# Inverse rows kept in a PSUM bank while VectorE updates them, with one PSUM bank fewer for the recurrence's transposes

## The chip, the core and the metric

The kernel runs on one core of a Trainium2 chip. A core has five engines, each with an instruction queue of its own that runs in order: TensorE (PE in the profile; PEld is its weight load), VectorE (DVE), ScalarE (ACT), GpSimd (POOL) and SyncE (SP), which here only issues DMAs. Tensors lie in device memory (HBM), in SBUF (128 partitions) or in PSUM, of which this kernel uses eight banks of 128 partitions with 512 float32 each. TensorE writes its results to PSUM, from which VectorE and ScalarE read them.

The metric is the device time of one execution in microseconds. Lower is better. The time before is the median of three timed runs; the profile is of a further execution.

## The reference, cut to what matters

One layer of a hybrid decoder for one sequence of 1024 tokens, model width 1024, all float32. A modulated RMSNorm feeds one input projection to 3360 columns, which serves two mixers: an RWKV-7 recurrence of 8 heads (64 wide) and latent attention of 8 heads. Their gated outputs go through one output projection, a residual and a last norm. The change lies in the recurrence:

```python
def step(state, inp):
    r_t, w_t, k_t, v_t, kk_t, a_t = inp
    sa = jnp.einsum('bhvk,bhk->bhv', state, kk_t)
    state = (state * w_t[:, :, None, :]
             - sa[..., None] * (kk_t * a_t)[:, :, None, :]
             + v_t[..., None] * k_t[:, :, None, :])
    y = jnp.einsum('bhvk,bhk->bhv', state, r_t)
    return state, y
...
y = group_norm_heads(y, lnx_w, lnx_b)
y = y + jnp.sum(rh * kh * r_k.astype(jnp.float32), axis=-1, keepdims=True) * vh
```

Within a chunk of 64 tokens the vectors `sa` of all tokens depend on one another through a lower triangular system with ones on its diagonal. Solving it chunk by chunk replaces the step from token to token, and needs the inverse of one 64 x 64 triangular matrix for each head and chunk.

## The kernel before, in words

**Units.** The recurrence is cut into eight units. A unit is one group of four heads (two pairs `a`, with two heads `s` in the halves of the 128 partitions) and a quarter of the sequence, 256 tokens, which is four chunks. So a unit has 16 combinations of head and chunk, and as many triangular matrices.

**Stages of a unit.** `prep` makes the decayed vectors: `kb` (keys and the removal vectors), `rq` (r and kk). `products` multiplies them on TensorE into the PSUM tiles `gps`; VectorE applies the triangular mask (line 584) and the 32 x 32 diagonal blocks, two per matrix and 32 in all, go to device memory. `invert` (line 613) loads them back so that each of the 128 partitions holds one block, each block being in four partitions, and inverts all 32 blocks at once. A partition keeps 8 of the 32 rows of its block's inverse in `W` (128 x 8 x 32), which starts as rows of the identity, loaded from the input `winit`. For each column `u` from 0 to 30 one VectorE instruction multiplies the `u` entry of each row with row `u` of the block into `wtmp` (line 625) and one subtracts the product from `W` (line 627): 62 instructions a unit, each depending on the one before. `W` then goes to device memory (line 630), `fetch` loads it back in two layouts, and `tmat` builds the off-diagonal block of the full 64 x 64 inverse T with two sets of small matmuls, through the PSUM tiles `y1ps` and `y2ps`. `turn_kb` and `turn_v` transpose the keys and values on TensorE, through the PSUM tiles `tps` and `vps`, and ScalarE copies them out (lines 601, 610, 611). `chain` is the recurrence over the four chunks: short matmuls with ScalarE copies `X`, `ST` and `S` between them. `post` normalises the result and transposes it (`ytps`, copied out by ScalarE in line 770).

**The eight PSUM banks** in this part: two with tag `mm` for the input projection, two with tag `rp` for `prep` and `products`, two with tag `rt`, which `tps`, `vps`, `y1ps`, `y2ps` and `ytps` take in turn (the last unit's `ytps` uses `mm`), and one each for `rc` and `ry`, the chain. A tile that takes a bank waits until the copies out of the tile that had it are done. Before the units begin, a first group of projection tiles borrows `mm`, `rc`, `ry` and both `rt` banks for its accumulators.

**Order of the work.** Stages of several units overlap: a loop over `n` walks through steps and calls the parts of the units at the step numbers in `PREP`, `PROD`, `TURN`, `FETCH`, `TMAT` and `POST`. Between them it issues "filler": the input projection, three matmuls of 128 x 128 x 512 at a time (lines 164 to 166, `mm3`), whose weights are split into a high and a low part by ScalarE and GpSimd (lines 156, 157). A planner then fixes at build time the order of instructions in each engine's queue, from the program's order, from priorities (`tc.high_priority`) and from its own estimates of durations. On the chip the queues run in that order, and each instruction waits for its inputs. Attention and the output projection follow and are not touched.

Of the kernel before, what the change touches and what calls it, by code (L numbers as in the profile page):

```python
# [17 lines left out]
F32 = mybir.dt.float32  # L18
# [3 lines left out]
AF = mybir.ActivationFunctionType  # L22
# [64 lines left out]
def hymba_kernel(ctx: ExitStack, tc: tile.TileContext, x, pos, cols, cst, winit, w_ada, b_gate, w_in, w_lora, w0,  # L87
# [157 lines left out]
    with ExitStack() as s0:  # L245
# [62 lines left out]
        for i in range(4, 8):  # L308
            load_x(i)
        ws.append(load_w(GROUP[2][0], P, st, 3, st))  # L310
        acc = [[(psM if m == 0 else psA).tile([P, HALF], F32, tag=t, name=f"acc{m}{h}", bufs=1 if m == 1 else 2)
                for h, t in enumerate(tags)] for m, tags in enumerate((("mm", "mm"), ("rc", "ry"), ("rt", "rt")))]
        seq = [(0, 0), (1, 0), (0, 1), (1, 1)] + [(kt, h) for kt in range(2, NK) for h in range(2)]
        modulation(0)
        turn_x(*seq[0])
# [276 lines left out]

    def turn_kb(un):

        ps = [psA.tile([P, 8, C], F32, tag="rt", name="tps") for _ in range(2)]
        for c in range(8):
            for s in range(2):
                rows = slice(s * 64, s * 64 + 64)
                T.transpose(ps[s][:, c, :], un["kb"][rows, c, :, :].rearrange("p a t -> p (a t)"), ident[rows, rows])
        for s in range(2):  # L600
            A.activation(un["KB"][:, s], ps[s][:], AF.Copy, scale=col("hs_b" if s else "hs_a"))

    def turn_v(un, q):

        qs = slice(q * 4, q * 4 + 4)
        ps = psA.tile([64, 4, P], F32, tag="rt", name="vps")
        for i in range(4):
            c = q * 4 + i
            T.transpose(ps[:, i, :], un["v"][:, c * C:(c + 1) * C], ident)
        A.copy(un["ST"][64:128, qs, 0, :], ps[:, :, 0:64])  # L610
        A.copy(un["ST"][0:64, qs, 1, :], ps[:, :, 64:128])

    def invert(un):

        i = un["n"]
        N = ch.tile([P, 32, 32], F32, tag="N", name="N", bufs=CB["N"])
        for q in range(4):
            SY.dma_start(N[q * 32:(q + 1) * 32], d_n[i][:])
        W = ch.tile([P, 8, 32], F32, tag="W", name="W")
        SY.dma_start(W[:].rearrange("p i t -> p (i t)"), winit)  # L620
        tp = ch.tile([P, 128], F32, tag="wtmp", name="wtmp")
        for u in range(31):
            n, m = u // 4 + 1, 31 - u
            t = tp[:, :n * m].rearrange("p (i t) -> p i t", i=n)
            V.tensor_tensor(t, W[:, 0:n, u:u + 1].to_broadcast([P, n, m]),  # L625
                            N[:, u:u + 1, u + 1:32].to_broadcast([P, n, m]), ALU.mult)
            V.tensor_tensor(W[:, 0:n, u + 1:32], W[:, 0:n, u + 1:32], t, ALU.subtract)  # L627
        d = d_w[i][:].rearrange("n (i q) t -> q n i t", q=4)
        for q in range(4):
            SY.dma_start(d[q], W[q * 32:(q + 1) * 32])  # L630

    def fetch(un):

# [12 lines left out]
    def tmat(un):  # L646

        GA, TT, T1 = un["GA"], un["TT"], un["T1"]
        ps = psA.tile([P, 8, 32], F32, tag="rt", name="y1ps")
        for c in range(8):  # L650
            for s in range(2):
                a = s * 64
                T.matmul(ps[a + 32:a + 64, c, :], lhsT=GA[s][c // 4][a:a + 32, c % 4, 32:64], rhs=T1[a:a + 32, c, :],
                         start=True, stop=True)
        Y1 = ch.tile([P, 8, 32], F32, tag="Y1", name="Y1")
        A.mul(Y1[32:64], ps[32:64], -1.0)
        V.tensor_scalar(Y1[96:128], ps[96:128], -1.0, None, ALU.mult)
        yield
        ps = psA.tile([P, 8, 32], F32, tag="rt", name="y2ps")
        for c in range(8):  # L660
            for s in range(2):
                a = s * 64
                T.matmul(ps[a:a + 32, c, :], lhsT=Y1[a + 32:a + 64, c, :], rhs=TT[a + 32:a + 64, c, 32:64],
                         start=True, stop=True)
        A.copy(TT[0:32, :, 32:64], ps[0:32])
        V.tensor_copy(TT[64:96, :, 32:64], ps[64:96])

        for q in range(2):
            A.copy(GA[0][q][0:64, :, 0:C], un["rq"][0:64, q * 4:q * 4 + 4, 0, :])
            A.copy(GA[1][q][64:128, :, 0:C], un["rq"][64:128, q * 4:q * 4 + 4, 0, :])  # L670
        yield
# [63 lines left out]
    def post(un):  # L735

        Y = un["Y"]
        ys = evp.tile([P, 8, C], F32, tag="p2", name="ys", bufs=2)
        A.copy(ys[:], Y[:])
        last = un["n"] == 7  # L740

        def fetched(nm, src):
            t = etile(nm) if last else evp.tile([P, HALF], F32, tag="p2", name=nm, bufs=2)
            for a, p, aq in pairs(un):
                SY.dma_start(t[:, aq], src[p][:, un["ts"]])
            return t


        early = [fetched("bv", d_bv), fetched("gr", d_gr)] if last else None
        s1 = evp.tile([P, 8], F32, tag="s1", name="s1")  # L750
        V.tensor_reduce(s1[:], ys[:], AX.X, ALU.add)
        V.tensor_scalar(s1[:], s1[:], 1.0 / C, None, ALU.mult)
        G.tensor_tensor(ys[:], ys[:], s1[:, :, None].to_broadcast([P, 8, C]), ALU.subtract)
        yield
        y2 = evp.tile([P, 8, C], F32, tag="p2", name="y2", bufs=2)
        A.activation(y2[:], ys[:], AF.Square)
        s2 = evp.tile([P, 8], F32, tag="s2", name="s2")
        V.tensor_reduce(s2[:], y2[:], AX.X, ALU.add)
        V.tensor_scalar(s2[:], s2[:], 1.0 / C, GN_EPS, ALU.mult, ALU.add)
        G.tensor_tensor(s2[:], s2[:], col("pw").to_broadcast([P, 8]), ALU.pow)  # L760
        G.tensor_tensor(ys[:], ys[:], s2[:, :, None].to_broadcast([P, 8, C]), ALU.mult)
        yield
        for q in range(2):
            p = 2 * un["g"] + q
            ps = (psM if last else psA).tile([64, 4, P], F32, tag="mm" if last else "rt", name="ytps")
            for i in range(4):
                T.transpose(ps[:, i, :], ys[:, q * 4 + i, :], ident)
            for s in range(2):
                rows = slice(s * 64, s * 64 + 64)
                A.activation(y2[rows, q * 4:q * 4 + 4, :], ps[:, :, rows], AF.Identity,  # L770
                             scale=col("lnx_w", 2 * p + s)[0:64], bias=col("lnx_b", 2 * p + s)[0:64])
            yield
        bv = early[0] if last else fetched("bv", d_bv)
        y2f = y2[:].rearrange("p c t -> p (c t)")
        G.tensor_tensor(y2f, bv[:], y2f, ALU.add)
        gr = early[1] if last else fetched("gr", d_gr)
        V.tensor_tensor(gr[:], y2f, gr[:], ALU.mult)
        for a, p, aq in pairs(un):
            SY.dma_start(d_y[p][:, un["ts"]], gr[:, aq])
        yield  # L780
# [605 lines left out]
```

## Time and profile before

| | us |
|---|---|
| median of three timed runs | 932.11 |
| the three runs | 941.20, 930.44, 932.11 |
| the profiled execution | 920.99 |
| its span, first to last instruction | 918.8 |
| busy in the span: PE, DVE, ACT, POOL | 835.3, 575.3, 476.5, 296.2 |

In the views, a group's row gives line, engine, operation, output and inputs by the program's names, the count, and durations in ns as minimum/median/maximum, then the first and last start in us. A row of the waits gives who waited for whom, us in total, the number of waits, the longest. A row of the timeline gives start, duration (us), and what ran. A row by stretch gives the stretch, its length, the busy time of each engine with its instruction count, then the granted TensorE clock (1 is full), the DMA share and GB/s; asked for one tile, it has VectorE's busy time for that tile alone. A row of the chain of waits in order of time gives start, duration, and what was on the chain.

### The profile page before, as it was taken

What the parts mean: (1) busy time and instruction counts of PE and PEld (TensorE: products, weight loads), DVE (VectorE), ACT (ScalarE), POOL (GpSimd) and SP (SyncE); (2) the same over time, 40 slices, a digit from 0 to 9 for tenths busy, and PEclk for the clock granted to TensorE, in tenths of its full rate; (3) what the DMA queues carried; (4) which work ended last, traced back from release to release, by engine and by line L of the source; (5) the groups of instructions that cost most, each with busy time, mean ns of one, the idle gap of its engine ahead of it and who ended that gap; (6) DMA issues with size and microseconds to landing.
All of it is one profiled execution on the core that took longest, in us unless ns stands there. A gap on an engine that the chain in (4) does not pass through costs nothing.

```text
span 918.8 us, 16567 instructions
## 1 busy us (share of the span) xinstructions
PE 835.3 (91%) x5812; PEld 641.2 (70%) x5812; DVE 575.3 (63%) x1462; ACT 476.5 (52%) x1112; POOL 296.2 (32%) x351
## 2 busy tenths in 40 slices
PE   1798997999999999898899999997799998989996
PEld 0586785776777777566667767765678777868885
DVE  5795349378495654955757366247778788765443
ACT  2655332444644636346245464554778888873311
POOL 1311423131232323423133122223436454454400
PEclk9999999999999999998999999999999999999998
DMA  8764433333435324435333254157102031017233
GB/s 253 247 194 153 140 110 115 95 105 88 134 118 150 118 69 135 121 69 165 118 99 104 65 151 139 49 172 203 55 18 70 21 110 59 1 56 239 85 126 126
DMA packets 131714, 106.66 MB, mean 116 GB/s; under 512 B 40616, under 2 KB 108464, under 8 KB 131632
## 3 DMA queue, kind: packets, MB, share of 16 engines
q1 hardware_dynamic: 130672, 102.46, 37.5%
q0 software_dynamic: 960, 3.15, 1.5%
q8 instruction: 46, 0.75, 0.3%
q14 instruction: 36, 0.29, 0.1%
HBM read 76.46 MB, written 29.10 MB: 115 GB/s over the span
## 4 chain that ended last, share of the span: by engine, by line
PE 66%; DVE 13%; ACT 9%; issue 4%; DMA 4%; POOL 2%; SPq 1%; POOLq 0%; DVEq 0%; ACTq 0%
PE mm L164 10%; PE mm L165 8%; PE mm L166 8%; PE po L1160 3%; PE po L1162 3%; PE po L1161 3%; PE gps L577 3%; ACT pr L1087 2%; DVE wtmp L625 2%; DVE W L627 2%; PE tp L1098 2%; ACT PTh L1107 1%; PE rc L712 1%; PE rc L694 1%; PE Y L728 1%
## 5 line engine op out<-in xcount | busy, mean ns | idle before, releaser
L164 PE MATMUL mm<-hTh,whi 128*128 128x512 f32 (+1 forms) x384 | 167.2, 435 | 3.1 <-DVE wtmp L625 2.3
L166 PE MATMUL mm<-hTh,wlo 128*128 128x512 f32 (+1 forms) x384 | 156.9, 409 | 0.0
L165 PE MATMUL mm<-hTl,whi 128*128 128x512 f32 (+1 forms) x384 | 156.8, 408 | 0.0
L157 POOL TENSOR_TENSOR wlo<-wraw,whi 128x512 fp32r<-128x512 f32 (+1 forms) x54 | 71.4, 1323 | 233.8 <-ACT whi L156 215.4
L164 PEld LDWEIGHTS mm<-hTh,whi 128*128 128x128 f32 (+1 forms) x384 | 73.3, 191 | 24.0 <-issue 3.1
L166 PEld LDWEIGHTS mm<-hTh,wlo 128*128 128x128 f32 (+1 forms) x384 | 73.2, 191 | 17.7
L165 PEld LDWEIGHTS mm<-hTl,whi 128*128 128x128 f32 (+1 forms) x384 | 73.5, 191 | 14.6 <-issue 1.4
L1091 POOL TENSOR_SCALAR pr<-pr,sm 128x512 f32<-128x512 f32 (+2 forms) x96 | 55.6, 588 | 72.4 <-DVE sm L1088 50.2
L627 DVE TENSOR_TENSOR W<-W,wtmp 128x60 f32<-128x60 f32 (+24 forms) x248 | 71.5, 288 | 5.8 <-DVE wtmp L625 0.3
L625 DVE TENSOR_TENSOR wtmp<-W,N 128x60 f32<-128x60 f32 (+24 forms) x248 | 69.2, 279 | 5.5
L156 ACT CAST whi<-wraw 128x512 fp32r<-128x512 f32 (+1 forms) x54 | 32.7, 607 | 59.4 <-PE mm L165 36.6
L720 ACT ACTIVATE ST<-rc,eL 64x64 f32<-64x64 f32 x120 | 37.1, 309 | 46.2 <-PE rc L712 44.5
L1087 ACT ACTIVATE pr<-sp,mx,rss 128x128 f32<-128x128 f32 (+3 forms) x64 | 53.3, 834 | 14.8 <-DVE mx L1080 12.3
L1108 DVE TENSOR_TENSOR PTl<-tp,PTh 128x512 fp32r<-128x512 f32 (+2 forms) x96 | 52.2, 553 | 11.8 <-ACT PTh L1107 10.1
L1079 DVE TENSOR_REDUCE mx<-sp 128x1 f32<-128x128 f32 (+3 forms) x64 | 48.0, 750 | 11.4 <-PE sp L1073 11.1
L1160 PE MATMUL po<-wo,yh 128*128 128x512 f32 x128 | 50.3, 393 | 0.8 <-ACT od L1134 0.8
L1107 ACT CAST PTh<-tp 128x512 fp32r<-128x512 f32 (+2 forms) x96 | 44.0, 477 | 13.1 <-PE tp L1098 10.2
L1098 PE MATMUL tp<-cstt,pr 128*128 128x128 f32 x288 | 45.0, 277 | 5.9 <-POOL pr L1091 2.9
L1162 PE MATMUL po<-wo,yl 128*128 128x512 f32 x128 | 50.3, 393 | 0.0
L1161 PE MATMUL po<-wo,yh 128*128 128x512 f32 x128 | 50.3, 393 | 0.0
L1119 PE MATMUL op<-PTh,Vt 128*128 128x256 f32 (+1 forms) x160 | 42.1, 293 | 5.1 <-ACT od L1134 5.1
L584 DVE TENSOR_TENSOR GA<-gps,cstt 128x512 f32<-128x512 f32 x32 | 21.4, 684 | 29.4 <-PE Y L728 22.6
(279 smaller groups left out, 1934.0 us busy)
## 6 DMA issues: line engine op xcount, KB each, us to landing
wraw<-in_w_in SPq DMA_DIRECT2D x52, 256.0 KB, 3.1
wa<-in_w_ada SPq DMA_DIRECT2D x64, 128.0 KB, 3.1
xt<-in_x SPq DMA_DIRECT2D x8, 512.0 KB, 7.4
wg<-in_w_ada SPq DMA_DIRECT2D x32, 128.0 KB, 2.5
N<-d_n SPq DMA_DIRECT2D x32, 128.0 KB, 3.1
wor<-in_w_out SPq DMA_DIRECT2D x16, 256.0 KB, 3.1
cr<-d_c SPq DMA_DIRECT2D x14, 256.0 KB, 3.4
d_c<-craw SPq DMA_DIRECT2D x10, 256.0 KB, 2.2
```

The lines of the kernel that those rows point to most:

```text
L157: G.tensor_tensor(lo[:, :, :m], raw[:, :, :m], hi[:, :, :m].bitcast(F32), ALU.subtract)
L164: T.matmul(ps[:m], lhsT=hi[:, k % 4, :m], rhs=a, start=first, stop=False)
L165: T.matmul(ps[:m], lhsT=hi[:, k % 4, :m], rhs=b, start=False, stop=False)
L166: T.matmul(ps[:m], lhsT=lo[:, k % 4, :m], rhs=a, start=False, stop=last)
L625: V.tensor_tensor(t, W[:, 0:n, u:u + 1].to_broadcast([P, n, m]), N[:, u:u + 1, u + 1:32].to_broadcast([P, n, m]), ALU.mult)
L627: V.tensor_tensor(W[:, 0:n, u + 1:32], W[:, 0:n, u + 1:32], t, ALU.subtract)
L1087: A.activation(pr[:, 0:n], sp[:, 0:n], AF.Exp, scale=rss[:, i:i + 1], bias=mx[:], accum_out=sm[:])
L1091: G.tensor_scalar(pr[:, a:e], pr[:, a:e], sm[:], 1.0, ALU.mult, ALU.mult)
L1098: T.transpose(tp[:, j, :], pr[:, (j0 + j) * P:(j0 + j + 1) * P], ident)
L1160: T.matmul(ps, lhsT=yh[k][:, ts_], rhs=hi, start=first, stop=False)
L1161: T.matmul(ps, lhsT=yh[k][:, ts_], rhs=lo, start=False, stop=False)
L1162: T.matmul(ps, lhsT=yl[k][:, ts_], rhs=hi, start=False, stop=last)
```

## The change

`W` moves to a PSUM bank with a tag `w` of its own. The start rows are loaded into an SBUF tile `Ws` and copied into `W` by ScalarE; the 62 VectorE instructions work on `W` in PSUM; ScalarE copies the finished rows back to `Ws`, from which they are stored. The bank comes from `rt`, which keeps one: `tps`, `vps`, `y1ps`, `y2ps` and `ytps` share it. `turn_kb` held two tiles at once and wrote them in alternation; it now makes one half of the partitions, copies it out, and then makes the other half. The first group's last accumulator takes the bank `w` instead of the second `rt` bank.

```diff
-        acc = [[(psM if m == 0 else psA).tile([P, HALF], F32, tag=t, name=f"acc{m}{h}", bufs=1 if m == 1 else 2)
-                for h, t in enumerate(tags)] for m, tags in enumerate((("mm", "mm"), ("rc", "ry"), ("rt", "rt")))]
+        acc = [[(psM if m == 0 else psA).tile([P, HALF], F32, tag=t, name=f"acc{m}{h}", bufs=1 if m else 2)
+                for h, t in enumerate(tags)] for m, tags in enumerate((("mm", "mm"), ("rc", "ry"), ("rt", "w")))]
...
     def turn_kb(un):
-        ps = [psA.tile([P, 8, C], F32, tag="rt", name="tps") for _ in range(2)]
-        for c in range(8):
-            for s in range(2):
-                rows = slice(s * 64, s * 64 + 64)
-                T.transpose(ps[s][:, c, :], un["kb"][rows, c, :, :].rearrange("p a t -> p (a t)"), ident[rows, rows])
         for s in range(2):
-            A.activation(un["KB"][:, s], ps[s][:], AF.Copy, scale=col("hs_b" if s else "hs_a"))
+            ps = psA.tile([P, 8, C], F32, tag="rt", name="tps", bufs=1)
+            rows = slice(s * 64, s * 64 + 64)
+            for c in range(8):
+                T.transpose(ps[:, c, :], un["kb"][rows, c, :, :].rearrange("p a t -> p (a t)"), ident[rows, rows])
+            A.activation(un["KB"][:, s], ps[:], AF.Copy, scale=col("hs_b" if s else "hs_a"))
...
     def turn_v(un, q):
-        ps = psA.tile([64, 4, P], F32, tag="rt", name="vps")
+        ps = psA.tile([64, 4, P], F32, tag="rt", name="vps", bufs=1)
...
     def invert(un):
-        W = ch.tile([P, 8, 32], F32, tag="W", name="W")
-        SY.dma_start(W[:].rearrange("p i t -> p (i t)"), winit)
+        W = psA.tile([P, 8, 32], F32, tag="w", name="W", bufs=1)
+        Ws = ch.tile([P, 8, 32], F32, tag="W", name="Ws")
+        SY.dma_start(flat(Ws), winit)
+        A.copy(W[:], Ws[:])
         tp = ch.tile([P, 128], F32, tag="wtmp", name="wtmp")
         for u in range(31):
...
             V.tensor_tensor(W[:, 0:n, u + 1:32], W[:, 0:n, u + 1:32], t, ALU.subtract)
+        A.copy(Ws[:], W[:])
         d = d_w[i][:].rearrange("n (i q) t -> q n i t", q=4)
         for q in range(4):
-            SY.dma_start(d[q], W[q * 32:(q + 1) * 32])
+            SY.dma_start(d[q], Ws[q * 32:(q + 1) * 32])
...
     def tmat(un):
-        ps = psA.tile([P, 8, 32], F32, tag="rt", name="y1ps")
+        ps = psA.tile([P, 8, 32], F32, tag="rt", name="y1ps", bufs=1)
...
-        ps = psA.tile([P, 8, 32], F32, tag="rt", name="y2ps")
+        ps = psA.tile([P, 8, 32], F32, tag="rt", name="y2ps", bufs=1)
...
     def post(un):
-            ps = (psM if last else psA).tile([64, 4, P], F32, tag="mm" if last else "rt", name="ytps")
+            ps = (psM if last else psA).tile([64, 4, P], F32, tag="mm" if last else "rt", name="ytps",
+                                            bufs=2 if last else 1)
```

## The prediction

> **What bounds the kernel now.** I read the page from the top: the engines' shares and the chain of waits, then the busy time of each engine by stretch.
>
> ```profile
> span 918.8 us, 16567 instructions
> PE 835.3 (91%) x5812; PEld 641.2 (70%) x5812; DVE 575.3 (63%) x1462; ACT 476.5 (52%) x1112; POOL 296.2 (32%) x351
> PE 66%; DVE 13%; ACT 9%; issue 4%; DMA 4%; POOL 2%; SPq 1%; POOLq 0%; DVEq 0%; ACTq 0%
> PE mm L164 10%; PE mm L165 8%; PE mm L166 8%; PE po L1160 3%; PE po L1162 3%; PE po L1161 3%; PE gps L577 3%; ACT pr L1087 2%; DVE wtmp L625 2%; DVE W L627 2%; PE tp L1098 2%; ACT PTh L1107 1%; PE rc L712 1%; PE rc L694 1%; PE Y L728 1%
> ...
> core 0: us, PE busy (x) PEld busy (x) DVE busy (x) ACT busy (x) POOL busy (x), PEclk, DMA share, GB/s
> 135.00:575.00 440.00, 420.89 (x3393) 307.77 (x3392) 279.96 (x816) 213.08 (x532) 125.99 (x112) 0.96 0.40 113
> ```
>
> The last row is the stretch in which all eight inversions lie. TensorE is busy for 420.9 of its 440 us, so it is the bound there: 19.1 us are idle, and a granted clock of 0.96 takes another 0.04 x 440 = 17.6 us. The 36.7 us together are the ceiling of anything that only takes waits away. VectorE is busy for 280 us and matters only where TensorE waits for it; still, the two lines of the inversion hold 4% of the chain.
>
> Next, those two lines by tile, and in the same stretch alone:
>
> ```profile
> L625 DVE TENSOR_TENSOR wtmp<-W,N x248: 155/213/1351, 135.0 to 567.0; 128x60 f32<-128x60 f32 x12, 128x54 f32<-128x54 f32 x8, 128x66 f32<-128x66 f32 x8, 128x28 f32<-128x28 f32 x8
> L627 DVE TENSOR_TENSOR W<-W,wtmp x248: 164/215/1332, 135.2 to 567.2; 128x60 f32<-128x60 f32 x12, 128x54 f32<-128x54 f32 x8, 128x66 f32<-128x66 f32 x8, 128x28 f32<-128x28 f32 x8
> 135.00:575.00 440.00, 140.67 (x496) 0.96 0.40 113
> ```
>
> Minimum, median and maximum: half of these instructions take about 0.214 us, some take 1.3. At the median, 496 would take 106.1 us; they took 140.7, so 34.5 us are stall (4.3 us an inversion). The timeline of VectorE with the GpSimd instruction of the same moment shows where a long one falls:
>
> ```profile
> 136.77 0.22 DVE L625 TENSOR_TENSOR wtmp<-W,N 128x54 f32<-128x54 f32 x1
> 137.02 0.22 DVE L627 TENSOR_TENSOR W<-W,wtmp 128x54 f32<-128x54 f32 x1
> 137.27 1.18 DVE L625 TENSOR_TENSOR wtmp<-W,N 128x52 f32<-128x52 f32 x1
> ...
> 137.04 1.33 POOL L157 TENSOR_TENSOR wlo<-wraw,whi 128x512 fp32r<-128x512 f32 x1 [1.25 <-ACT whi L156]
> ```
>
> The 52-element multiply begins inside GpSimd's subtraction (137.04 to 138.37) and ends at 138.45, just behind it. Is that a matter of where its operands lie? VectorE groups with one input in PSUM against one with both in SBUF:
>
> ```profile
> L584 DVE TENSOR_TENSOR GA<-gps,cstt x32: 669/682/693, 116.2 to 524.2; 128x512 f32<-128x512 f32 x32
> L565 DVE TENSOR_TENSOR bv<-bps,v x8: 672/690/693, 153.0 to 492.1; 128x512 f32<-128x512 f32 x8
> L796 DVE TENSOR_TENSOR yl<-yr,yh x12: 675/692/1785, 751.6 to 837.9; 128x512 fp32r<-128x512 f32 x12
> ```
>
> Forty with a PSUM input never exceed 0.693 us; the SBUF pair reaches 1.785. After the change both inversion lines have W in PSUM and one SBUF input, so I expect their maximum to fall to about 0.25 us and VectorE to lose the 34.5 us.
>
> **What the relief is worth.** TensorE's waits in the stretch, then three spots where its granted clock was down:
>
> ```profile
> PE gps L577 <- DVE W L627: 5.6, 1, 5.6
> PE mm L164 <- DVE wtmp L625: 2.3, 1, 2.3
> PE gps L577 <- DVE kb L555: 1.8, 2, 1.4
> PE gps L577 <- DVE wtmp L625: 1.6, 2, 1.2
> ...
> PE gps L577 <- DVE kb L554: 1.2, 1, 1.2
> ...
> PE vps L609 <- ACT y L770: 0.6, 1, 0.6
> ...
> PE ytps L767 <- ACT ST L611: 0.3, 1, 0.3
> ...
> 156.00:163.00 7.00, 4.83 (x21) 4.25 (x22) 5.75 (x19) 0.00 (x0) 0.11 (x1) 0.52 0.53 154
> 439.00:443.00 4.00, 2.97 (x7) 2.42 (x8) 3.76 (x14) 0.22 (x2) 0.00 (x0) 0.58 0.53 189
> 549.00:556.00 7.00, 6.55 (x23) 4.99 (x20) 6.59 (x20) 4.88 (x13) 2.57 (x2) 0.52 0.52 168
> ```
>
> The five waits on W, wtmp and kb sum to 12.5 us. I count kb (the decayed keys) too, because its instructions share VectorE's queue with the inversion and shift with it. What is late next is GpSimd's half of kb or a DMA of r, so I take 10 of the 12.5. The clock: 7 x 0.48 + 4 x 0.42 = 5.1 us are lost in the first two spots, both next to a wait (5.6 and 2.3 us); the third row is as low with TensorE busy for 6.55 of 7 us, so waits aren't all of it, and I take 3. Gain: 13 us.
>
> **What W in PSUM adds.** First, the price of VectorE's access. No VectorE instruction writes PSUM in this trace. Reads can be compared, 8 elements each, from PSUM (rn) and from SBUF (s):
>
> ```profile
> L512 DVE TENSOR_SCALAR rn<-nps x8: 152/166/167, 93.4 to 473.0; 128x8 f32<-128x8 f32 x8
> L752 DVE TENSOR_SCALAR s<-s x8: 153/171/172, 228.6 to 622.4; 128x8 f32<-128x8 f32 x8
> ```
>
> 166 against 171 ns: the read costs nothing. For the write I take zero too, as the row for reads is the nearest; the other end is the price at which nothing is left of the relief, 34.5 us / 496 = 70 ns an instruction, and a gain of the 5 ns seen here (2.5 us in all) is the end below. [...]
>
> Second, two ScalarE copies of 128x256 an inversion (start rows in, finished rows out). The nearest rows, with the queue row that says how early the planner places what needs the finished W:
>
> ```profile
> L669 ACT COPY GA<-rq x16: 390/405/407, 175.3 to 581.4; 64x256 f32<-64x256 f32 x16
> L656 ACT ACTIVATE Y<-y1ps x8: 375/376/377, 175.7 to 580.0; 32x256 f32<-32x256 f32 x8
> SPq L630 <- DVE W L627: 8.3, 4, 5.6
> ```
>
> 16 x 0.4 = 6.4 us of ScalarE, which has 227 us free in the stretch. The first copy needs only the loaded start rows and hides ahead of the inversion. The second lengthens each inversion by about 0.4 us against the 4.3 it saves. But it is also a wait in ScalarE's queue: behind it stand the X, ST and S copies of the recurrence, and TensorE's chain matmuls wait for those. SyncE's queue, where the stores of W stand today, waited 8.3 us for W in all. With VectorE 4.3 us earlier most of that goes; I charge 1 us, between 0 and 8.3. SyncE's loads and stores stay as many; the stores now wait for the copy. If this cover went, the whole 8.3 would be paid.
>
> **What one bank for the turns costs.** Per unit eight tiles use it: two of keys, two of values, two of T (y1ps, y2ps) and two of norm (ytps, not in the last unit). Each must now wait until the tile just before it has been copied out, not the one before that. With two banks TensorE waited 0.6 + 0.3 = 0.9 us for such copies (the vps and ytps rows above). The close pairs are the second keys, values and norm tile, 3 a unit; at the 0.3 us of the one such wait, 24 would cost 7.2 us; filler matmuls placed in between can make it 0. I take 2, nearer to the two-bank row, as TensorE is the late engine and ScalarE mostly waits for it. [...]
>
> The keys' transposes also change order: today they alternate between the two partition halves, afterwards eight of one half follow each other.
>
> ```profile
> 126.32 0.71 PE L599 MATMUL tps<-cstt,kb 64*128 64x64 f32 x16
> 593.61 0.87 PE ytps L767 x8
> ```
>
> Alternating, 16 take 0.71 us (44 ns each). Norm's transposes, 128 columns wide and all of one kind, take 0.87 / 8 = 109 ns; at half the width 54 ns, 16 x 54 = 0.87 us. That is +0.16 us a unit, 1.3 us in eight; at the full 109 ns it would be 8.3 us. I take 2. The first group's accumulator in the w bank has been emptied before the first inversion: zero; if not, the first start copy waits, not TensorE.
>
> **Sum.** Gain 10 + 3, cost 1 + 2 + 2: 8 us less. The profiled execution took 920.99 us (2.2 around its span), so 913. The three timed runs are higher, with a median of 932.11 (930.44 to 941.20); 8 off the median is **924 us**, 0.9% less.
>
> **Rivals.**
>
> *Faster by more* (0.17). The relief clears the waits whole and, with a steadier TensorE, most of the low clock as well: 12.5 + half of 17.6 = 21.3 us, less about 1 of cost: 912. For it: VectorE's long instructions sit on the chain. Against: in most of the stretch TensorE has no wait, and the clock is as low at 549 us without any of these waits.
>
> *Slower by over 2%* (0.12). ScalarE's copy of the finished W is planned earlier than VectorE delivers it; all recurrence copies behind it wait, and TensorE, in order, behind those. SyncE's longest wait for W was 5.6 us. At 4 us in each of eight inversions it is 32 us, less the 13: 951. It decides from about 1.6 us an inversion, where it eats up the gain. For it: the chain has little else to run on ScalarE's queue. Against: the relief itself brings VectorE forward.
>
> *PSUM is dear for VectorE* (0.10): 70 ns an instruction or so, the relief is used up, the 5 us of costs stay: 937. For it only the unknown write; against it the reads.
>
> *The stalls stay* (0.06): the long instructions are not due to SBUF inputs, and W in PSUM is held up as before: again 937.
>
> **Numbers.** The forecast has 0.55. Faster by over 2% (below 913.5) is the first rival, 0.17; slower by over 2% (above 950.8) the second, 0.12; within 2%, about what a measurement of this kernel can tell from no change, the rest, 0.71. The forecast's own ends: the whole gain, 12.5 + 5.1, without cost, 914; and half the gain, 6.5, against 17.5 of cost (of the upper ends' 8.3 + 7.2 + 8.3 = 23.8, three quarters), 943. To hold 8 in 10 I reach into the first rival and to its value of 912, and no further than 943 above, since the second rival is mostly beyond: 908 to 943, the 4 us below 912 for PSUM writes that are cheaper than SBUF's and other waits moving along.
>
> **What would show it.** L625 and L627 with a maximum near 0.25 us and a sum of about 106 us; no wait of TensorE for W or wtmp; PEclk above 0.52 where the 5.6 us wait was; ScalarE's waits for W under 2 us in all; TensorE's waits for KB, ST and y copies at some 2 us. I am wrong if the median of L627 rises by tens of ns, if ScalarE waits for W by several us an inversion, or if the waits on VectorE vanish and the span stays, because the order of TensorE's work was the limit.

## The result, and the profile after

The changed kernel took 942.49 us in the median, the kernel before 932.11; the ratio of their runs is 1.014 (95% interval 1.0105 to 1.0175). It is slower, by less than 2%; I had said 0.9% faster. The profiled execution took 936.33 us. From its page, the span, the engines' shares and the chain by engine:

```profile
span 934.1 us, 16586 instructions
...
PE 853.0 (91%) x5812; PEld 656.7 (70%) x5812; DVE 550.8 (59%) x1462; ACT 483.0 (52%) x1128; POOL 296.2 (32%) x351
...
PE 73%; ACT 9%; DVE 7%; issue 4%; DMA 4%; POOL 2%; SPq 1%; POOLq 0%; DVEq 0%; ACTq 0%
```

VectorE lost 24.5 us of work (575.3 to 550.8) and its share of the chain fell from 13% to 7%. TensorE, with the same 5812 matmuls, is busy 17.7 us longer. The two lines of the inversion, now 627 and 629, in the changed kernel's groups by tile (ns: minimum/median/maximum):

```profile
L627 DVE TENSOR_TENSOR wtmp<-W,N x248: 155/210/238, 137.5 to 583.0; 128x60 f32<-128x60 f32 x12, 128x54 f32<-128x54 f32 x8, 128x66 f32<-128x66 f32 x8, 128x28 f32<-128x28 f32 x8
L629 DVE TENSOR_TENSOR W<-W,wtmp x248: 164/218/246, 137.7 to 583.2; 128x60 f32<-128x60 f32 x12, 128x54 f32<-128x54 f32 x8, 128x66 f32<-128x66 f32 x8, 128x28 f32<-128x28 f32 x8
```

And its timeline of GpSimd and of VectorE at one of GpSimd's subtractions (start, duration):

```profile
139.53 1.28 POOL L157 TENSOR_TENSOR wlo<-wraw,whi 128x512 fp32r<-128x512 f32 x1 [1.25 <-ACT whi L156]
...
140.03 0.22 DVE L629 TENSOR_TENSOR W<-W,wtmp 128x52 f32<-128x52 f32 x1
140.29 0.21 DVE L627 TENSOR_TENSOR wtmp<-W,N 128x50 f32<-128x50 f32 x1
140.53 0.22 DVE L629 TENSOR_TENSOR W<-W,wtmp 128x50 f32<-128x50 f32 x1
```

Nothing takes longer than 0.246 us any more (1.351 before), and inside GpSimd's subtraction VectorE runs on at 0.22 us. This part of the prediction came true to the figure. The medians, 210 and 218 ns against 213 and 215, show that VectorE pays nothing here for writing PSUM, within 3 ns. The waits of the changed kernel from 135 to 620 us that bear on the change:

```profile
DVE wtmp L627 <- ACT W L622: 14.2, 2, 10.6
...
PE gps L577 <- DVE kb L554: 5.2, 1, 5.2
...
ACT Ws L630 <- DVE W L629: 4.9, 3, 3.6
...
PE nps L509 <- ACT dg L382: 2.9, 1, 2.9
...
PE kps L536 <- ACT sq L515: 2.4, 1, 2.4
```

TensorE's waits for W and wtmp are gone but for 0.5 us, but others have come in their place (the last two rows are not among the waits before), and over the whole span TensorE is idle for 81.1 us where it was idle for 83.5. ScalarE waits 4.9 us for the finished W. VectorE waits 14.2 us for the start copy, which I had said would hide. So TensorE waits about as long as before, and what makes the span longer is that it is busy for 17.7 us more. The stretch of the inversions (the last of them now runs on until 583 us), by engine, and below it for TensorE's projection tiles (mm) alone, shows where it is:

```profile
135.00:575.00 440.00, 421.13 (x3319) 310.91 (x3318) 249.35 (x791) 213.44 (x533) 123.65 (x110) 0.93 0.39 111
```

```profile
135.00:575.00 440.00, 242.49 (x873) 0.93 0.39 111
```

TensorE is as busy as before (421.1 against 420.9 us), yet ran 3319 matmuls instead of 3393, 873 of them projection matmuls instead of 911: the granted clock is 0.93, not 0.96. For the whole program I split each run's span into span x mean granted clock ("at full clock") and the rest ("lost to clock"). It is bookkeeping: a low clock while TensorE waits counts as lost although it costs nothing, so the two can shift against each other by some us. Means over the runs that the comparisons use, which leave out runs over 1.5% above the fastest of their kernel (one of the changed kernel's eleven took 1308.91 us, at a granted clock of 0.56):

| kernel | ratio to before, 95% | span | at full clock | lost to clock |
|---|---|---|---|---|
| before (five groups of runs) | 1 | 924.3 to 928.6 | 891.2 to 892.0 | 33.1 to 36.6 |
| after | 1.014 (1.0105, 1.0175) | 940.1 | 891.1 | 49.0 |
| e1 bank alone | 1.0107 (1.0064, 1.0150) | 936.8 | 901.3 | 35.5 |
| e2 before, no scaling | 0.9990 (0.9939, 1.0041) | 925.0 | 892.9 | 32.1 |
| e3 after, no scaling | 1.0012 (0.9976, 1.0047) | 926.6 | 888.9 | 37.7 |
| e4 after, scaling in rp | 1.0121 (1.0043, 1.0198) | 939.0 | 889.0 | 50.0 |
| e5 order put back | 1.0211 (1.0136, 1.0285) | 947.2 | 888.2 | 59.0 |
| e6 bank and copies | 1.0218 (1.0177, 1.0259) | 949.2 | 897.7 | 51.5 |
| e7 keys half by half | 1.0012 (0.9976, 1.0049) | 929.1 | 892.0 | 37.1 |
| e8 matmuls in the hole | 1.0140 (1.0089, 1.0191) | 941.7 | 896.7 | 45.0 |
| e9 matmuls in every unit | 1.0228 (1.0174, 1.0281) | 950.1 | 917.6 | 32.5 |
| e10 start copy on VectorE | 1.0071 (1.0027, 1.0115) | 935.2 | 892.4 | 42.9 |
| e11 both copies on VectorE | 1.0150 (1.0058, 1.0243) | 936.5 | 890.9 | 45.7 |
| e12 before, no GpSimd reads | 0.9797 (0.9727, 0.9866) | 905.1 | 879.7 | 25.4 |
| e13 start copy, later scaling | 1.0032 (0.9993, 1.0070) | 927.9 | 891.8 | 36.1 |
| e14 after, no GpSimd reads | 0.9955 (0.9909, 1.0001) | 923.0 | 882.5 | 40.5 |
| e15 bank, no GpSimd reads | 0.9790 (0.9744, 0.9835) | 908.0 | 891.2 | 16.8 |
| e16 split on VectorE | 0.9966 (0.9927, 1.0005) | 923.9 | 884.8 | 39.1 |

The groups ran on different chips, and the kernel before differs by 4 us between them. So the ratios, each to the kernel before of its own group, are safer than differences of spans.

At full clock the change costs nothing (891.1 us); by this split the clock accounts for the whole loss, 49.0 against some 35. In the two traces, from 40 us to the tail of the program, TensorE falls to half clock 11 times after the change and 9 times before, but it stays there for 82 us instead of 41. The longest low stretch is just behind the fifth inversion, at the scaling of the compressed keys and values (`scale_ckv`, four 128-column matmuls at line 388 for each half). Rows of the changed kernel by engine, then, in a fence of their own, TensorE's projection tiles alone in the last three of these stretches:

```profile
404.90:408.30 3.40, 3.02 (x21) 2.19 (x19) 3.22 (x9) 2.07 (x5) 1.22 (x3) 1.00 0.58 167
408.30:411.70 3.40, 0.92 (x9) 0.95 (x9) 2.66 (x5) 3.23 (x9) 3.22 (x3) 1.00 0.38 87
411.70:425.10 13.40, 7.65 (x37) 6.70 (x39) 8.39 (x13) 2.49 (x5) 7.09 (x7) 0.51 0.60 159
425.10:442.60 17.50, 15.55 (x157) 12.67 (x156) 7.77 (x27) 8.66 (x25) 0.00 (x0) 0.50 0.10 34
```

```profile
408.30:411.70 3.40, 0.00 (x0) 1.00 0.38 87
411.70:425.10 13.40, 0.00 (x0) 0.51 0.60 159
425.10:442.60 17.50, 1.05 (x2) 0.50 0.10 34
```

After one stretch with TensorE almost idle (0.92 of 3.4 us) the clock halves, and it stays at half for about 31 us, although TensorE is busy for 15.55 of the last 17.5. What is missing there is wide matmuls: two projection matmuls in 34 us. Before the change the scaling, from 416 to 428 us, met no more projection work, but the hole was shorter. By engine, and below it for the projection tiles:

```profile
412.00:431.00 19.00, 15.50 (x138) 12.48 (x135) 7.74 (x24) 15.18 (x43) 3.39 (x4) 0.82 0.47 151
```

```profile
412.00:431.00 19.00, 0.45 (x2) 0.82 0.47 151
```

Two projection matmuls in 19 us, at a clock of 0.82: half clock lasted 6.8 us there. Half of 30.7 against half of 6.8 is 12 us, more than half of the 20 us by which the two traces differ in time lost to the clock.

### The profile page after: what moved, and what is told of

It is laid out like the page before. It is cut to its first block, busy times and chain, and to the rows that moved or that the text cites. A ratio compares the mean times of both kernels' runs of the same rounds, so it can differ in the third digit from the quotient of the medians.

```text
span 934.1 us, 16586 instructions
## 1 busy us (share of the span) xinstructions
PE 853.0 (91%) x5812; PEld 656.7 (70%) x5812; DVE 550.8 (59%) x1462; ACT 483.0 (52%) x1128; POOL 296.2 (32%) x351
## 4 chain that ended last, share of the span: by engine, by line
PE 73%; ACT 9%; DVE 7%; issue 4%; DMA 4%; POOL 2%; SPq 1%; POOLq 0%; DVEq 0%; ACTq 0%
PE mm L164 10%; PE mm L165 9%; PE mm L166 9%; PE po L1164 3%; PE po L1166 3%; PE po L1165 3%; PE gps L577 3%; ACT pr L1091 2%; PE rc L715 2%; PE tp L1102 2%; PE Y L728 2%; PE rc L697 2%; PE rc L712 2%; PE Y L731 2%; ACT PTh L1111 1%
## 5 line engine op out<-in xcount | busy, mean ns | idle before, releaser
L627 DVE TENSOR_TENSOR wtmp<-W,N 128x60 f32<-128x60 f32 (+24 forms) x248 | 51.4, 207 | 20.5 <-ACT W L622 14.2
L723 ACT ACTIVATE ST<-rc,eL 64x64 f32<-64x64 f32 x120 | 37.1, 309 | 40.0 <-PE rc L715 38.3
L629 DVE TENSOR_TENSOR W<-W,wtmp 128x60 f32<-128x60 f32 (+24 forms) x248 | 53.3, 215 | 5.5
```

## The experiments

Five causes were to be told apart. **Hole**: the scaling leaves TensorE without projection matmuls at the fifth inversion. **Bank**: one bank for the turns makes TensorE wait. **Order**: the planner, which works from its own estimates, moved T's first matmuls (`y1ps`) back among the projection matmuls. **Copies**: the two ScalarE copies. **Clock**: small matmuls without wide ones between them lower the granted clock, wherever they come from.

**One part at a time.** e7 is the kernel before with only the keys' order changed; e1 has everything but `W` in PSUM; e6 has the copies too, with `W` copied into and out of a further SBUF tile.

```diff
 # e7, against before: the loop of the change in turn_kb, two banks kept
-        ps = [psA.tile([P, 8, C], F32, tag="rt", name="tps") for _ in range(2)]
...
+            ps = psA.tile([P, 8, C], F32, tag="rt", name="tps")
...
 # e1, against after: W loaded, kept and stored in SBUF
-        W = psA.tile([P, 8, 32], F32, tag="w", name="W", bufs=1)
-        Ws = ch.tile([P, 8, 32], F32, tag="W", name="Ws")
-        SY.dma_start(flat(Ws), winit)
-        A.copy(W[:], Ws[:])
+        W = ch.tile([P, 8, 32], F32, tag="W", name="W")
+        SY.dma_start(W[:].rearrange("p i t -> p (i t)"), winit)
...
-        A.copy(Ws[:], W[:])
...
 # e6, against after: W in SBUF, both copies kept
-        W = psA.tile([P, 8, 32], F32, tag="w", name="W", bufs=1)
+        W = ch.tile([P, 8, 32], F32, tag="Wk", name="W")
```

> The kernel before with its two banks and W in SBUF; only the keys' transposes are ordered as after the change, eight of one half of the partitions and then eight of the other. If the 1.1% of the bank alone are due to the lost alternation, this takes 936 to 940; if they are due to waiting for the one bank, or to the order that the planner makes of it, 929 to 932 (1.3 us of TensorE more).

> The loss of the bank alone: W stays in SBUF as before, without the two ScalarE copies; one bank serves the turns of keys, values, T and norm, and the keys are turned half by half. Three theories on the 1.4%. HOLE: the loss is made where scale_ckv holds both projection banks and TensorE has no projection matmul (407.5 to 441.5 us, with the granted clock halved for 30.7 us), because the planner put other work there; the change gains elsewhere. BANK: waiting for the one bank costs everywhere. COPY: W in PSUM and its copies cost. HOLE expects 928 to 938 (no relief, no long hole; the long VectorE instructions up to 1.3 us are back); BANK at least 945, as the bank's cost stands without the relief; COPY 932.

> One bank for the turns and both ScalarE copies, but W stays in SBUF (the copies go from one SBUF tile to another and back). ORDER expects the time of the bank alone, 936 to 941, as the copies hardly move the order (y1ps at 273, 407, 530, 630, 766, 853, 956, 1087); COPY expects 945 or more: the copies themselves are the cost and the relief pays for part of it.

e1's median of 938.82 lies just above HOLE's range and below BANK's; e6's 950.8 is what COPY had said. By the ratios, on 930 us: the keys' order costs 1 us (not distinguishable from none), the bank with it 10, the copies 10 more, and `W` in PSUM gives 7 back: 13 in all. Each step is uncertain by some 5 us. The bank's 10 stand at full clock (901.3 against 891.2). They are not waits for copies out of the bank, as I had priced them; TensorE's waits in e1:

```profile
PE gps L577 <- DVE W L627: 8.2, 2, 5.6
PE gps L577 <- DVE wtmp L625: 4.0, 3, 2.3
PE mm L164 <- DVE wtmp L625: 2.7, 1, 2.7
...
PE ytps L768 <- ACT y L771: 1.2, 2, 0.8
...
PE vps L608 <- ACT y L771: 0.6, 2, 0.4
...
PE tps L599 <- ACT KB L600: 0.2, 1, 0.2
```

Copies out hold TensorE up for 2.0 us, near my charge of 2. But the unrelieved inversion now costs 14.9 us of waits where it cost 9.5. These rows do not add up to 10. I take the rest to lie in the order that the planner chose; no run shows it. In e6 the copies' loss is clock: 51.5 us lost against 35.5 in e1.

**The hole.** e2 and e3 leave the scaling out of the kernel before and after; e4 gives its tile another bank.

```diff
 # e2, e3
-                yield from scale_ckv()
+                for _ in range(6):
+                    yield
 # e4
-            ps = psM.tile([P, HALF], F32, tag="mm", name="rps")
+            ps = psA.tile([P, HALF], F32, tag="rp", name="rps")
```

> The kernel before, leaving out the scaling of the key/value latent (scale_ckv: its matmuls, its reloads and its stores); its empty steps stay. This is the reference for the next run. HOLE expects some 10 us less than before, 922, since the 19.5 us without projection matmuls (411 to 430.5 us) close; BANK and COPY expect about 930, as the scaling itself is only 16 matmuls, 8 us of ScalarE and VectorE.

> The changed kernel, leaving out the same scaling of the key/value latent. HOLE expects it below the kernel before without scaling by the predicted gain of some 8 us: about 914, with no stretch of half clock longer than 10 us. BANK and COPY expect it above that kernel by the same 10 to 13 us as with the scaling: about 940.

> The changed kernel with the scaling's PSUM tile (rps) in the banks of prep and products (tag rp) in place of the projection's two banks (tag mm), so that the projection's next tile need not wait for it. HOLE expects 920 to 928: the stretch without projection matmuls is gone or short, and the half clock with it. BANK and COPY expect 940.

Without the scaling the changed kernel is level with the one before (1.0012), and the kernel before gains nothing (0.9990): almost the whole loss hangs on the change and the scaling together. HOLE had said more, 922 and 914 us; the medians are 929.31 and 928.01, so the relief does not show without the scaling either. The bank of its tile is not what matters (e4: 50.0 us lost to clock, as after).

**T's order put back.** In e5 projection matmuls are held behind `y1ps` where they stood before, to within three projection matmuls.

```diff
+                    with held_back():
                         mm3(ps, m, w, slice(h * HALF, (h + 1) * HALF), k, k == 0, k == NK - 1)
```

> The changed kernel, with one thing added: the projection's matmuls are made to stand behind T's first matmuls (y1ps) of a unit in TensorE's queue, at the places where y1ps stood before the change (behind projection matmul 272, 401, 525, 624, 741, 856, 956 and 1087; the change had moved them to 288, 450, 573, 657, 768, 858, 965 and 1104). Only the order in the queue changes; no instruction is added. ORDER: the 1.4% come from where the planner puts T's matmuls and what follows, because it takes the inversion in PSUM for longer; small matmuls then lie together, the granted clock halves there, and the hole at the scaling is deep. It expects 920 to 928 (the relief of 8 us less what the bank costs), fewer than 45 us at half clock (85 after, 41 before). BANK expects 938 as without the relief; COPY 940.

That made it worse, 59.0 us lost. The row of the same stretch, with fewer matmuls still:

```profile
135.00:575.00 440.00, 420.34 (x3249) 304.91 (x3248) 247.90 (x768) 208.23 (x520) 118.86 (x107) 0.90 0.38 105
```

ORDER had said 920 to 928. So the place of T among the projection matmuls is not the cause by itself. Whether the order of the other instructions is, stays open: I could not hold all of it as it was.

**Wide matmuls added.** e8 and e9 put extra 512-column matmuls, whose results nothing uses, into `prep` and `products`: 30 in one unit, 133 in seven.

```diff
+        if un["n"] in (1, 2, 3, 4, 5, 6, 7):
+            for _ in range(n):
+                T.matmul(ps, lhsT=hTh[0][:, 0:P], rhs=hTh[0][:, 0:HALF], start=True, stop=True)
```

> The changed kernel with 30 more matmuls of 128x128x512, whose results nothing reads, written into PSUM tiles of prep and products of the seventh unit just ahead of their real content; they stand in the hole at the scaling (408 to 442 us), where TensorE waits for 10 us in all. They are pure extra work: 30 x 0.228 = 6.8 us at full clock. Nothing else in TensorE's order moves. CLOCK (the theory that is left: with few 512-column matmuls in an interval of some 3.4 us the granted clock halves, and it comes back only where they fill more than half of one) expects the half clock of 30.7 us in the hole to fall below 15 us and the whole time to fall in spite of the extra work, to 930 to 938. If the clock is only the mark of a slow stretch and not its cause, the time rises by up to 6.8 us: 944 to 949.

> The same in seven units: 19 such matmuls a unit, 133 in all, 30.3 us of extra TensorE work at full clock, part of it in TensorE's waits. The planner's order changes with it (y1ps at 273, 403, 531, 630, 759, 858, 964, 1104). CLOCK expects a mean granted clock of at least 0.965 against 0.948, so some 15 us back, and a time of 930 to 950 by how much of the 30.3 us lies in waits; without CLOCK it is 955 to 972.

Thirty did little: 45.0 us lost instead of 49.0, for 5.6 at full clock. CLOCK's forecast for them failed: a time of 930 to 938 and under 15 us of half clock in the hole, where the median is 944.64 and the half clock lasts 30.7 us as in the changed kernel. The rows of e8 by stretch:

```profile
410.50:417.30 6.80, 6.80 (x26) 6.03 (x25) 2.23 (x5) 0.62 (x1) 2.73 (x2) 0.50 0.55 118
417.30:424.10 6.80, 4.95 (x27) 3.73 (x25) 4.71 (x6) 2.00 (x4) 4.31 (x5) 1.00 0.66 192
424.10:448.00 23.90, 23.60 (x181) 18.70 (x182) 8.15 (x28) 9.66 (x27) 0.00 (x0) 0.50 0.14 46
```

The clock came back only for 417 to 424 us, where sixteen of the added matmuls stand close together; behind them it fell again, with TensorE busy for 23.60 of 23.90 us. That the clock comes back only where wide matmuls fill more than half of some 3.4 us, as the theory had it, is not so in the kernel before: there it came back at 429.3 us (0.99 in the next 3.4 us) behind 3.4 us at 0.50 without one projection matmul. With 133 added matmuls the loss falls to 32.5, less than the kernel before has, for 26.5 us of added work. The clock, 0.966 in the mean, is what CLOCK had said; the time, 952.05 in the median, lies above its 930 to 950. The rows of e9 by stretch, up to 575 us and for the spot of the hole:

```profile
135.00:575.00 440.00, 432.90 (x3376) 315.80 (x3377) 238.15 (x755) 205.22 (x510) 120.56 (x106) 0.97 0.37 105
...
408.00:442.00 34.00, 33.90 (x269) 24.81 (x267) 14.27 (x36) 16.07 (x41) 7.47 (x6) 0.85 0.35 90
```

0.97 where the changed kernel has 0.93, and 0.85 from 408 to 442 us where it has 0.56: with 133 more wide matmuls the clock was higher. They fill TensorE's waits as well (7.1 us idle up to 575 us, 18.9 in the changed kernel), so e9 does not tell wide matmuls from a busy TensorE; e8's last row, busy and at half clock, does. As a remedy e9 costs more than it saves.

**The copies elsewhere.** e10 makes the start copy on VectorE, e11 both copies; e13 is e10 with the scaling four tiles later.

```diff
 # e10, e11, e13
-        A.copy(W[:], Ws[:])
+        V.tensor_copy(W[:], Ws[:])
 # e11
-        A.copy(Ws[:], W[:])
+        V.tensor_copy(Ws[:], W[:])
 # e13
-            if i == 16:
+            if i == 20:
                 yield from scale_ckv()
```

> The changed kernel with the copy of the start rows into W made by VectorE, which needs it, in place of ScalarE; VectorE waited 14.2 us for that copy in two inversions. T's matmuls keep their places (y1ps at 288, 450, 573, 670, 768, 858, 965, 1103). If that wait is on the path, 928 to 936; if not, 938 to 946.

> The changed kernel with both copies of the inverse (start rows in, finished rows out) on VectorE instead of ScalarE; the planner keeps T's first matmuls where the changed kernel has them (within 20 of 1104 instructions). COPY theory (copies queued on ScalarE put TensorE's small matmuls into clusters and so lower the clock): the time lost to clock falls from 49 us to about 35, full-clock time 891 plus at most 5 for VectorE's 16 copies: 926 to 932, a ratio of 0.995 to 1.00. SPREAD theory (the clock is lost where the planner leaves TensorE without projection matmuls, whatever engine copies): 938 to 946, 1.007 to 1.015, lost to clock 43 to 50.

> The changed kernel with the start copy on VectorE (as in e10) and the scaling of the compressed keys and values planned four tiles later, so that its small matmuls no longer meet the fifth inversion's. If the placement of the scaling makes the loss that e10 left (43 us lost to clock): 30 to 36 lost, full-clock time 888 to 893, 920 to 928, a ratio of 0.987 to 0.998. If the clusters only move elsewhere, as when its tile changed banks (e4): 933 to 941, 1.004 to 1.013.

e10 wins half of the loss back, e11 none for certain (its interval is wide), e13 most of it: 36.1 us lost to clock, against 33.1 for the kernel before beside it. A copy in ScalarE's queue is thus not the cause by itself: COPY had said at most 1.00 for e11, and its interval begins at 1.0058. What the scaling's later place gains alone is not shown, as the intervals of e10 and e13 overlap, and in e13's trace a long stretch at half clock has moved along with the scaling, which now runs from 509 to 528 us:

```profile
510.70:538.00 27.30, 21.11 (x172) 15.85 (x169) 10.60 (x31) 10.27 (x30) 3.99 (x4) 0.50 0.51 151
```

Its other stretches at half clock from 40 us on are shorter, 41 us in all against 51. e13 is the change almost without its loss, and it is no faster than the kernel before.

**What the relief is worth.** GpSimd's subtraction (line 157) is replaced by a fill with zeros in the kernel before (e12), after (e14) and with the bank alone (e15); e16 makes it on VectorE.

```diff
 # e12, e14, e15
-            G.tensor_tensor(lo[:, :, :m], raw[:, :, :m], hi[:, :, :m].bitcast(F32), ALU.subtract)
+            G.memset(lo[:, :, :m].bitcast(F32), 0.0)
 # e16
-            G.tensor_tensor(lo[:, :, :m], raw[:, :, :m], hi[:, :, :m].bitcast(F32), ALU.subtract)
+            V.tensor_tensor(lo[:, :, :m], raw[:, :, :m], hi[:, :, :m].bitcast(F32), ALU.subtract)
```

> The kernel before, with GpSimd's subtraction that makes the low parts of the weights replaced by a fill with zeros: the low parts are left out of the result, the matmuls with them still run. Where GpSimd's reads of SBUF cause the stalls of VectorE's inversion lines (two inputs in SBUF): the maximum of the two lines falls from 1.35 us to about 0.3, their sum over the inversions from 140.7 us to 105-115, and TensorE's waits for W, wtmp and kb go. The time then shows what that relief is worth without any PSUM bank being moved: about 10 us less at full clock by the changed kernel against the bank alone, so 918 to 926, unless the clock takes it back. Where the stalls have another cause, the maximum stays above 1 us and the time within 4 us of the kernel before.

> The changed kernel with GpSimd's subtraction for the low parts of the weights replaced by a fill with zeros, as in e12; the low parts are left out of the result. The stalls that the change removes are then mostly gone already in e12, so what the change still does is its one bank, its copies and its order. If the bank is dear by itself (10 us as in e1): full-clock time 888 to 892, as much as the changed kernel has with these reads, and 933 to 942 with some 45 lost to clock. If the bank is dear only while VectorE stalls: full-clock time 878 to 883, 916 to 932 with 38 to 49 lost to clock.

> The bank alone (e1: keys, values, T and norm in one bank, W in SBUF) with the same fill with zeros in place of GpSimd's subtraction. If the bank is dear by itself: full-clock time 889 to 893 (e12's 879.7 + 10), 914 to 920. If it is dear only while VectorE stalls: 879 to 883, 903 to 910, as fast as e12.

> The kernel before with the subtraction for the low parts on VectorE instead of GpSimd; nothing is left out. VectorE gets 54 instructions of about 0.68 us (the price of its other 128x512 subtractions), 36.7 us in all, some 20 of them beside the inversions, and loses about 22 us of stalls, as in e12. If what e12 won (11.5 us at full clock, 8 of clock) came from VectorE's stalls: 908 to 920. If VectorE's queue is now the late one (the subtractions stand between the inversion's steps and wait for ScalarE's casts): 925 to 940.

In e12 the two lines, from the costliest groups of its page (busy us, mean ns):

```profile
L627 DVE TENSOR_TENSOR W<-W,wtmp 128x60 f32<-128x60 f32 (+24 forms) x248 | 61.0, 246 | 5.8 <-DVE wtmp L625 0.3
...
L625 DVE TENSOR_TENSOR wtmp<-W,N 128x60 f32<-128x60 f32 (+24 forms) x248 | 57.4, 231 | 5.5
```

And its timeline of VectorE and of GpSimd, beside what GpSimd still reads:

```profile
130.51 1.11 DVE L627 TENSOR_TENSOR W<-W,wtmp 128x69 f32<-128x69 f32 x1
131.65 1.21 DVE L625 TENSOR_TENSOR wtmp<-W,N 128x66 f32<-128x66 f32 x1
132.90 1.33 DVE L627 TENSOR_TENSOR W<-W,wtmp 128x66 f32<-128x66 f32 x1
...
130.26 1.26 POOL L544 TENSOR_TENSOR rq<-r,E 128x512 f32<-128x512 f32 x1
131.49 2.64 POOL L547 TENSOR_TENSOR kb<-kw,Ei 64x512 f32<-64x512 f32 x2
```

The sum falls from 140.7 to 118.4 us, 22.3 of the 34.5, and the long ones that are left, up to 1.326 us where I had said 0.3, stand beside GpSimd's other multiplications. Beside the fill alone, which reads nothing, 35 instructions of the inversion ran, none longer than 0.228 us. So the stalls here are GpSimd's reads, with the subtraction making most of them. Where the operands lie decides whether these two lines are held up: with both inputs in SBUF they reach 1.351 us in the kernel before, 1.348 in e6 and 1.326 in e12, and with `W` in PSUM, in the changed kernel, 0.246 us at most. How one engine holds up the other no run shows.

The time of e12, 19 us less, is not the price of those stalls, as I had expected. The same fill wins 17 us in the changed kernel (940.1 to 923.0), which has no such stalls, and e16, which stops the same reads but gives VectorE the subtractions to do, wins only 2 (its interval reaches 1), although its two lines, at 120.8 us, lose nearly as much of their stalls as in e12. A fill is shorter than the subtraction and, as the rows of GpSimd before and in e14 show, no longer waits for ScalarE's cast:

```profile
L157 POOL TENSOR_TENSOR wlo<-wraw,whi 128x512 fp32r<-128x512 f32 (+1 forms) x54 | 71.4, 1323 | 233.8 <-ACT whi L156 215.4 <-DMA d_k<-pst 9.0 <-DMA wa<-in_w_ada 4.3
```

```profile
L157 POOL MEMSET wlo<- 128x512 f32 (+1 forms) x54 | 27.7, 518 | 254.0 <-PE mm L166 231.1 <-PE acc L166 22.5 <-POOLq L1382 0.3
```

Low parts of the weights that are ready sooner may be the cause; no run tells that from the rest. What the change does where the subtraction's reads are gone can be read: 0.9797 to 0.9955, some 15 us slower, nearly all of it clock (25.4 to 40.5 us). And the bank alone costs nothing there by the ratios (0.9797 and 0.9790; 3 us by the spans), though its split says +11.5 at full clock and -8.6 of clock. By the total the bank is dear only while VectorE stalls, by the split it is dear by itself; I trust the total, and leave the split of e15 open. No kernel that computes everything is faster than the one before beyond doubt.

## Why the prediction was wrong, step by step

- **The stalls** go because W is in PSUM: right. Maximum 0.246 us (said: near 0.25); the two lines over the whole program 104.7 us (said: about 106). e6, with the same copies and `W` in SBUF, still has 1.348 us.
- **PSUM is free for VectorE**, taken at zero against the rival with 70 ns: right for these instructions, 218 against 215 and 210 against 213 ns.
- **The relief**, 10 us of waits: the waits on W and wtmp went, all but 0.5 us, but what came late next was a wait for VectorE's own kb (5.2 us on line 554, 1.2 before), which I had counted among those that go. TensorE's idle time from 135 to 575 us is 18.9 us, and was 19.1: I had taken only some 2.5 of the 12.5 us to come back as other waits, and by the trace they nearly all did. Measured as the step from e6 to the changed kernel the relief is 7 us against 10, or 13 with the clock's share: right in kind, too high.
- **The start copy "hides ahead of the inversion"**: wrong. VectorE waited 14.2 us for it in two inversions, as the copy stands in ScalarE's in-order queue behind other work. (The 10.6 us are the fifth inversion's: its copy ran at 370.6 us, behind ScalarE's copies of results that TensorE, at half clock from 360.7, delivered late.) I had charged only the finished W's copy (1 us), where ScalarE's waits are 4.9 us. Together the copies cost 10 us (e1 to e6), half of which e10 wins back.
- **One bank, 2 us, and keys in halves, 2**: the keys cost 1 (e7), the bank with them 10 (e1). I looked at the direct waits for copies out, which are indeed 2 us, and missed that with fewer banks the unrelieved inversion holds TensorE longer (14.9 us against 9.5). The end of 7.2 us was nearer by luck, as it was made of waits for copies out. (Two slips in these sums change nothing: the close pairs are 23, as the last unit's norm tile lies in `mm`, and three quarters of 23.8 is 17.9.)
- **The clock, 3 us of gain**: the step that failed. I tied the low clock to waits on VectorE and took it to improve with them. Where the 5.6 us wait had been it did (1.00 from 150 to 180 us), but over the program it got worse by some 14 us: TensorE is left for longer with small matmuls alone, the worst of it at the scaling (30.7 us at half clock against 6.8). The runs show this; which of the new instructions makes the planner order the work so stays open. My third clock row, low at 549 us with TensorE busy 6.55 of 7, was the hint that waits are not the cause, and I gave it a sentence instead of a term.
- **The rivals**: ScalarE's queue behind the finished W did not decide (4.9 us in three waits, not 4 an inversion). The stated way to be wrong that came true is the last: the waits on VectorE vanish and the span stays, because of the order of TensorE's work. I had given it no chance and no price. That 942.49 us still lies within 908 to 943 is luck: the upper end was made of waits for copies, keys and banks, not of clock.

The steps from run to run (bank, copies, relief) and the split into full clock and lost clock are two ways to cut the same 21 us between 8 less and 13 more; they do not add up.

## What to carry to other kernels

Where TensorE is busy for over nine tenths, look at the granted clock before counting waits, and at how the wide matmuls lie between the small ones; an edit that only shifts the order can lose more there than it saves in waits (here some 14 us of clock, while TensorE's idle time fell from 83.5 to 81.1 us). A kernel whose order comes from a planner should be measured with each part of a change alone: here one part gained 7 us, and two that looked like 1 and 4 cost 10 each. A spot where filler runs out is worth a look; shifting it by four tiles moved 27.3 us of low clock with it (e13).

## What the hardware showed that I had not expected

The clock halves although the trace shows TensorE busy throughout. Rows of the changed kernel by engine, then TensorE's projection tiles alone in the same stretches:

```profile
353.90:357.30 3.40, 3.40 (x71) 2.24 (x71) 0.43 (x1) 2.47 (x7) 0.00 (x0) 1.00 0.00 0
357.30:360.70 3.40, 3.40 (x37) 2.79 (x29) 0.92 (x4) 1.71 (x6) 1.76 (x2) 1.00 0.64 194
360.70:364.10 3.40, 3.40 (x23) 2.17 (x22) 0.00 (x0) 1.75 (x4) 2.07 (x2) 0.50 0.45 126
364.10:367.50 3.40, 3.40 (x30) 2.65 (x28) 0.00 (x0) 0.85 (x2) 0.00 (x0) 0.50 0.10 32
```

```profile
353.90:357.30 3.40, 1.97 (x5) 1.00 0.00 0
357.30:360.70 3.40, 0.66 (x3) 1.00 0.64 194
360.70:364.10 3.40, 1.24 (x2) 0.50 0.45 126
364.10:367.50 3.40, 0.00 (x0) 0.50 0.10 32
```

From 353.9 to 367.5 us TensorE is busy in every stretch. In the second one only 0.66 of 3.4 us went to 512-column matmuls; the next is at half clock, and it stays there while their share stays low (1.24 and 0.00 us in the next two). In the traces of the kernel before and of the changed one all 21 and all 25 changes of the granted clock lie on a grid of 3.413 us, and the stretches at half clock shown above, of 6.8, 23.9, 27.3 and 30.7 us, are 2, 7, 8 and 9 of its steps. At the scaling the clock fell behind a stretch with TensorE almost idle (0.92 of 3.4 us); in these rows it falls with TensorE busy for all of the 3.4 us before.

But a lack of wide matmuls does not always do it. In the kernel before, no projection matmul ran in these two stretches, and TensorE was idle for 0.7 us of each, yet the clock held:

```profile
414.20:417.60 3.40, 2.70 (x24) 2.07 (x25) 1.29 (x2) 3.36 (x11) 1.27 (x1) 1.00 0.53 195
417.60:421.00 3.40, 2.69 (x30) 2.36 (x29) 0.17 (x1) 2.86 (x7) 1.64 (x1) 1.00 0.95 283
```

What sorts the 3.4-us steps better is how many columns TensorE streams (the last number of a matmul's input in the timeline: 512 for a projection matmul), whether in wide matmuls or in many small ones. I counted them for the matmuls begun in each 3.41-us step, on the grid on which the clock changes, in all eighteen traces from 40 us to 15 us before the end. After 4096 columns or more, as many as eight projection matmuls, the next step was never at half clock (0 of 3606; in the traces of the kernel before and the changed one 0 of 404); after fewer than 2048 it was in 143 of 153 (15 of 16 in those two); in between, in 217 of 815 (21 of 88). So in these traces a step with under 2048 columns nearly always cost the clock, and one with 4096 always kept or regained it. This is a count and not an experiment: how the chip measures activity no run shows, and columns are not told apart from other measures of work.
